# The second attention by pairs of heads: masking by a matrix product, values with tokens on the partitions

## The chip, the cores and the metric

The kernel runs on one core of one Trainium2 chip. The metric is the device time of one execution, in microseconds, as the median of several executions. Work is shared by five engines that run side by side, each in the order of its own queue: TensorE (PE in the profile, with PEld for its weight loads), VectorE (DVE), ScalarE (ACT), GpSimd (POOL) and the DMA queues that SyncE (SP) and GpSimd issue. They wait for each other by semaphores.

## The reference, cut to what matters

The program is a trunk of two decoder layers over 256 tokens of width 1024, all in float32. Layer A uses differential attention, layer B "forgetting attention" over keys, values and forget gates that were computed once between the layers. Each layer has a SwiGLU feed-forward network before and after its attention. The change concerns layer B's attention alone:

```
def forgetting_attention(h, w_q, w_o, k, v, F):
    q = (h @ w_q).reshape(b, s, B_HEADS, HEAD_DIM)       # 16 heads of 64
    ...
        decay = Fq[..., None] - F_k[:, :, None, :]       # a number per query less one per key
        logits = einsum('bqhd,bkhd->bhqk', qb, k) * scale + decay
        logits = where(causal, logits, -inf)
        p = softmax(logits)
        return einsum('bhqk,bkhd->bqhd', p, v)
    ...
    return o.reshape(b, s, B_WIDTH) @ w_o
```

The tokens are taken in two blocks of 128 queries. The first block sees 128 keys and the second 256, so a head has 384 columns of scores on 128 partitions (`QT` in line 820 holds these two stretches).

## The kernel before, in words

**Layout and number format.** Activations lie with features on the partitions and tokens in the columns. A projection is done in split form: a weight piece and an activation are each cut into a high part, rounded to the format float32r, and a low part, and `mm3` (line 398) adds three products (high by high, low by high, high by low). Such a product of 256 columns is one matmul instruction; a product of plain float32 operands is two. Weight pieces of 128 x 1024 are loaded by SyncE, rounded by ScalarE (`cp_part`, line 288; `wh` in the profile) and subtracted by VectorE (`sub_part`, line 298; `wl`).

**Order of the work.** `InOrder` (line 58) wraps TensorE, ScalarE, VectorE and SyncE: instructions of each stay in the order in which the Python code issues them. It keeps a rough clock of each engine, and by that puts weight roundings and subtractions into gaps that it expects (`fill_act`, `fill_dve`, `bg`). GpSimd is called directly.

**The stage around the change.** `late_pairs` (line 498) computes the first two tiles of queries, each with four heads (`lp` in the profile), while normalisation of the input still runs; its last steps are the normalised input `HH`, `HL`, and then the second query tile (`lcol`, `lt`, `q`) on ScalarE and VectorE. Then `attention_b` (line 1059) goes head by head, in 19 turns of a pipeline, 16 heads and three turns to empty it:

- `decay(t + 1)`: VectorE adds the query's number, the key's number (a row broadcast by DMA, `fkb`) and the causal mask, for the next head.
- `normal(t - 1)`: VectorE takes the reciprocals of the sums (`rsb`) and divides the 384 columns of weights of the previous head.
- `scores(t)`: two products of 64 rows (`sb`), on VectorE scaled logits with the decay and the maximum (`nmb`), on ScalarE exponentials with their sums.
- `weights_t(t - 2)`: three transposes of the weights (`pwb`), copied to SBUF by ScalarE into one of two buffers (`wtb`).
- `values(t - 3)`: two products with features on the partitions (`pob`), two heads in one accumulator; after the second, ScalarE rounds it (`obh`) and VectorE subtracts (`obl`).

Between these, `step(n)` gives TensorE filler work by a written plan (`PLAN`, line 45): first the projection of the other two query tiles (`pair_proj`, `pq`, six matmuls a step), then the output projection of the heads that are done (`OutProj.steps`, `pw`, three matmuls a step). In the first turns a filler stands on both sides of the scores. `op.finish` (line 697) does the last two of eight parts of the output projection and updates the residual stream; the next feed-forward network starts with `lg` and `lu`.

Accumulators are PSUM tiles with tags: `sbank` has two buffers, `abank` and `bbank` one each, `mmbank` four.

Of the kernel before, what the change touches and what calls it, by code (L numbers as in the profile page):

```python
# [10 lines left out]
F32 = mybir.dt.float32  # L11
F32R = mybir.dt.float32r
BF16 = mybir.dt.bfloat16
AF = mybir.ActivationFunctionType
ALU = mybir.AluOpType
PSUM = bass.MemoryType.PSUM

P = 128
D = 1024
S = 256  # L20
NC = D // P
HD = 64
AH = 8
BH = 16
# [5 lines left out]
BIG = 3.0e38  # L30
# [9 lines left out]
CP_FIT = 0.9  # L40
DVE_FIT = 0.6
NFILL = 1
FRONT = 0
TAIL = 4
PLAN = [1, 1, 1, 1, 2, 1, 2, 3, 1, 3]
PACE = [0.62, 0.74, 0.62, 0.38, 0.76, 0, 0.74]
NRAW = 6
NLO = 5
# [59 lines left out]
def trunk(ctx, tc, a, out):  # L108
    nc = tc.nc
    InOrder.ready = {}  # L110
    pe = InOrder(tc, nc.tensor, 0.0, 1 / 2350)
    act = InOrder(tc, nc.scalar, 0.13, 1 / 1200)
    dve = InOrder(tc, nc.vector, 0.08, 1 / 960)
    sp = InOrder(tc, nc.sync, 0.0, 1 / 704)
    cp_ = ctx.enter_context(tc.tile_pool(name="cp", bufs=1))
# [3 lines left out]
    kp = ctx.enter_context(tc.tile_pool(name="kp", bufs=2))  # L119
    pp = ctx.enter_context(tc.tile_pool(name="pp", bufs=1, space=PSUM))  # L120

    def mmbank(name):
        return pp.tile([P, 512], F32, tag="mm", name=name, bufs=4)

    def sbank(name):
        return pp.tile([P, 512], F32, tag="s", name=name, bufs=2)

    def abank(name):
        return pp.tile([P, 512], F32, tag="ta", name=name)

    def bbank(name):
        return pp.tile([P, 512], F32, tag="tb", name=name)

    mm = pe.matmul
# [248 lines left out]
    def run_laters():  # L383
        for e in list(laters):
            e[0] -= 1
            if e[0] <= 0:
                laters.remove(e)
                e[1]()
# [9 lines left out]
    def mm3(ps, w, xx, first, last):  # L398
        (wh, wl), (xh, xl) = w, xx
        mm(ps, wh, xh, start=first, stop=False, skip_group_check=True)  # L400
        mm(ps, wl, xh, start=False, stop=False, skip_group_check=True)
        mm(ps, wh, xl, start=False, stop=last, skip_group_check=True)
        work(P)
# [329 lines left out]
    def pair_proj(src, dst, name):  # L733

        pq = mmbank(name)
        blk = take(src)
        for k in range(NC):
            for b in range(2):
                mm3(pq[:, b * 256:b * 256 + 256], blk(k * 256 + b * P), hn[k],
                    k == 0 and b == 0, k == NC - 1)  # L740
            if k == NC - 1:
                act.copy(dst, pq)
            yield k, NC
# [76 lines left out]
    QT = ((0, 128), (128, 256))  # L820
# [4 lines left out]
    ident, cmask, ub, skew, nlam, subg = (late[n] for n in ("ident", "cmask", "ub", "skew", "nlam", "subg"))  # L825
# [159 lines left out]
    op = attention_a()  # L985
# [5 lines left out]
    kT = [cp_.tile([P, 512], F32, name=f"kT{j}") for j in range(4)]  # L991
    vb = [[cp_.tile([P, 512], F32, name=f"vb{t}{nh}") for nh in range(2)] for t in range(2)]
# [17 lines left out]
    pz = sbank("pzf")[:, :S]  # L1010
# [13 lines left out]
    for i, (kk, n) in enumerate(v_proj("wkv", vb)):  # L1024
# [9 lines left out]
        if i == 3:  # L1034
# [4 lines left out]
            Fq = cp_.tile([P, 72], F32, name="Fq")[:, :2 * BH]  # L1039
# [6 lines left out]
            fdram = tc.dram_tile([BH, S], F32, name="fdram")  # L1046
# [12 lines left out]
    def attention_b():  # L1059
        ohs = [cp_.tile([P, 512], F32R, tag=f"hidh{j}", name=f"obh{j}") for j in range(4)]  # L1060
        ols = [cp_.tile([P, 512], F32R, tag=f"hidl{4 + j}", name=f"obl{j}") for j in range(4)]
        o = [(ohs[c // 2][:, (c % 2) * 256:(c % 2) * 256 + 256],
              ols[c // 2][:, (c % 2) * 256:(c % 2) * 256 + 256]) for c in range(NC)]
        q = [cp_.tile([P, 512], F32, tag=f"hidl{j}", name=f"q{j}") for j in range(4)]
        gs, ds, sms = {}, {}, {}

        def load_g(hd):
            g = cp_.tile([P, S], F32, tag=("hidh10", "hidl10", "hidl8", "hidl9")[hd % 4], name=f"fkb{hd}")
            nc.gpsimd.dma_start(g, bass.AP(fdram.tensor, fdram.offset + hd * S, [[0, P], [1, S]]))
            gs[hd] = g  # L1070

        def decay(hd):
            d = cp_.tile([P, 384], F32, tag=f"hidh{4 + hd % 4}", name=f"d{hd}")
            for qt, (c0, w) in enumerate(QT):
                dve.scalar_tensor_tensor(
                    d[:, c0:c0 + w], gs[hd][:, :w], Fq[:, qt * BH + hd:qt * BH + hd + 1], cmask[:, S - w:],
                    op0=ALU.add, op1=ALU.add)
            ds[hd] = d
            if hd + 4 < BH:
                load_g(hd + 4)  # L1080

        late_pairs("wq", q[:2], ((1, 4), (1, 3)), AF.Exp)
        for hd in range(4):
            load_g(hd)
        decay(0)
        op = OutProj(o)
        st = {}
        pob = {}
        mode[0] = "fill"

        def scores(hd):
            c, m = hd // 2, hd % 2
            rows = slice(m * HD, m * HD + HD)
            cb = (c % 2) * 256
            d = ds[hd]
            s = sbank(f"sb{hd}")
            for qt, (c0, w) in enumerate(QT):
                mm(s[:, c0:c0 + w], q[c // 2][rows, cb + qt * P:cb + qt * P + P],
                   kT[c // 2][rows, cb:cb + w], start=True, stop=True)
            nm = kp.tile([P, 2], F32, tag="nm", name=f"nmb{hd}")  # L1100
            sm = kp.tile([P, 2], F32, tag="sm", name=f"smb{hd}")
            for qt, (c0, w) in enumerate(QT):
                dve.tensor_tensor_reduce(
                    d[:, c0:c0 + w], s[:, c0:c0 + w], d[:, c0:c0 + w], -0.125, BIG,
                    ALU.add, ALU.min, accum_out=nm[:, qt:qt + 1])
                act.activation(d[:, c0:c0 + w], d[:, c0:c0 + w], AF.Exp,
                               bias=nm[:, qt:qt + 1], scale=-1.0, accum_out=sm[:, qt:qt + 1])
            sms[hd] = sm

        def normal(hd):  # L1110
            d = ds[hd]
            rs = kp.tile([P, 2], F32, tag="rs", name=f"rsb{hd}")
            dve.reciprocal(rs, sms[hd])
            for qt, (c0, w) in enumerate(QT):
                dve.tensor_scalar(d[:, c0:c0 + w], d[:, c0:c0 + w], rs[:, qt:qt + 1], None, op0=ALU.mult)

        def weights_t(hd):
            pw = abank(f"pwb{hd}")
            for b in range(3):
                pe.transpose(pw[:, b * P:b * P + P], ds[hd][:, b * P:b * P + P], ident)  # L1120
            wt = cp_.tile([P, 384], F32, tag=f"hidh{8 + hd % 2}", name=f"wtb{hd}")
            act.copy(wt, pw[:, :384])
            st[hd] = wt

        def values(hd):
            c, m = hd // 2, hd % 2
            rows = slice(m * HD, m * HD + HD)
            if m == 0:
                pob[c] = bbank(f"pob{c}")
            po, wt = pob[c], st[hd]  # L1130
            vs = slice((hd % 8) * HD, (hd % 8) * HD + HD)
            v0, v1 = vb[0][hd // 8][:, vs], vb[1][hd // 8][:, vs]
            mm(po[rows, 128:256], v1, wt[:, 256:384], start=True, stop=False, skip_group_check=True)
            mm(po[rows, 0:256], v0, wt[:, 0:256], start=False, stop=True, skip_group_check=True)
            if m == 1:
                oh, ol = o[c]
                act.copy(oh, po[:, :256])
                dve.tensor_tensor(ol, po[:, :256], oh.bitcast(F32), op=ALU.subtract)

        def fills():  # L1140
            for j in (2, 3):
                yield from pair_proj("wq", q[j], f"pq{j}")
            for _ in range(6):
                yield from op.steps()

        fill = fills()

        def step(n):
            for _ in range(n):
                next(fill, None)  # L1150

        step(FRONT)
        for t in range(BH + 3):
            n0, n1 = PLAN[2 * (t // 4):2 * (t // 4) + 2]
            step(n0)
            if t + 1 < BH:
                decay(t + 1)
            if 0 <= t - 1 < BH:
                normal(t - 1)
            if t < BH:  # L1160
                scores(t)
            step(n1)
            if 0 <= t - 2 < BH:
                weights_t(t - 2)
            if 0 <= t - 3 < BH:
                values(t - 3)
        for i, n in fill:
            if i % 4 == 3:
                run_laters()
        return op  # L1170

    pace[0] = PACE[5]
    op = attention_b()
    op.finish((1, 5), ((1, 7), (1, 6)))
    pace[0] = PACE[6]
# [132 lines left out]
```

## Time and profile before

| | |
|---|---|
| median of 3 executions | 1008.04 us (1007.78 to 1008.06) |
| the profiled execution's own time | 1012.33 us |
| its span in the trace | 1010.4 us |
| TensorE busy | 98% of the span |
| VectorE, ScalarE, GpSimd busy | 81%, 56%, 4% |
| second attention, from the first filler after the late pairs to the next network's first matmul | 738.90 to 812.39 us |

Times in the rows below are microseconds from the start of the span, and the second number of a row is its duration, unless the text says otherwise. "x6" counts instructions that were merged into the row. A bracket at the end of a row gives the idle time of the engine before it and the engine and tile whose end released it. Nearly all instructions go through the wrapper, so their line is that of the wrapper, L103, and rows are told apart by the tile that they write (left of the arrow). Matmuls are pipelined, so the pace is read from start to start and not from their durations.

### The profile page before, as it was taken

The numbers are of one execution on the slowest core, as the hardware profiler recorded it, in microseconds if no ns is written. First come the engines' busy times: TensorE is split into PE (matmuls) and PEld (weight loads), VectorE is DVE, ScalarE is ACT, GpSimd is POOL, SyncE is SP. The second block draws the span as 40 slices with busy tenths as digits, with TensorE's granted clock in tenths as the row PEclk, the third lists the DMA queues.
The fourth block names the chain that finished last, engine by engine and source line by source line (L and its number), as shares of the span: only waits on it lengthen the run. The fifth ranks groups of instructions, "written<-read, shape, count | busy, mean of one in ns | idle before, by whom it ended". The sixth has DMA issues, their size and how long they took to land.

```text
span 1010.4 us, 20397 instructions
## 1 busy us (share of the span) xinstructions
PE 986.9 (98%) x8076; PEld 948.1 (94%) x8076; DVE 821.5 (81%) x1379; ACT 562.3 (56%) x922; POOL 38.1 (4%) x64
## 2 busy tenths in 40 slices
PE   6999999999999999999999999999999999999996
PEld 4999999988999999999988999999977799999996
DVE  7989979899889998888798989889897697554553
ACT  4465455576767645455566544545665585544552
POOL 0000100001111000000000000000011010000000
PEclk9999999999999999999999999999999999999999
DMA  9988999958665899788767999989743337554551
GB/s 353 414 323 301 345 368 337 363 191 321 210 225 186 268 393 349 276 292 313 262 230 276 357 349 349 334 296 346 257 121 108 126 128 230 186 188 138 173 170 42
DMA packets 68129, 265.06 MB, mean 262 GB/s; under 512 B 7961, under 2 KB 8113, under 8 KB 57922
## 3 DMA queue, kind: packets, MB, share of 16 engines
q1 hardware_dynamic: 65810, 258.31, 72.2%
q0 software_dynamic: 1792, 4.81, 1.7%
q8 instruction: 63, 1.03, 0.4%
q10 hardware_dynamic: 432, 0.64, 0.2%
q14 instruction: 32, 0.26, 0.1%
HBM read 262.66 MB, written 2.65 MB: 263 GB/s over the span
## 4 chain that ended last, share of the span: by engine, by line
PE 91%; ACT 4%; DVE 3%; issue 1%; POOL 1%; DMA 0%; SPq 0%; DVEq 0%; ACTq 0%
PE po L103 24%; PE pg L103 21%; PE pu L103 21%; PE pf L103 5%; PE pv L103 4%; PE pw L103 3%; PE lp L103 3%; PE pk L103 1%; ACT nl L103 1%; PE pob L103 1%; PE lg L103 1%; PE lu L103 1%; PE pqk L103 1%; PE sb L103 1%; ACT on L103 1%; DVE ada L103 1%
## 5 line engine op out<-in xcount | busy, mean ns | idle before, releaser
L103 DVE TENSOR_TENSOR wl<-raw,wh 128x1024 fp32r<-128x1024 f32 (+1 forms) x368 | 400.9, 1105 | 90.4 <-issue 24.3
L103 ACT CAST wh<-raw 128x1024 fp32r<-128x1024 f32 (+1 forms) x368 | 349.2, 958 | 208.1 <-PE pu L103 95.0
L103 DVE CUSTOM_DVE_ANT_0 ada<-ada,cact,vecs 128x1024 f32<-128x1024 f32 x160 | 203.6, 1279 | 0.0
L103 PE MATMUL po<-hidl,wh 128*128 128x256 f32 x704 | 195.2, 277 | 0.0
L103 PE MATMUL po<-hidh,wh 128*128 128x256 f32 x704 | 195.2, 277 | 0.0
L103 PE MATMUL po<-hidh,wl 128*128 128x256 f32 x704 | 195.2, 277 | 0.0
L103 PE MATMUL pg<-HH,wh 128*128 128x256 f32 x608 | 168.8, 278 | 0.0
L103 PE MATMUL pu<-HH,wl 128*128 128x256 f32 x608 | 168.8, 278 | 0.0
L103 PE MATMUL pg<-HL,wh 128*128 128x256 f32 x608 | 168.7, 278 | 0.0
L103 PE MATMUL pu<-HH,wh 128*128 128x256 f32 x608 | 168.7, 278 | 0.0
L103 PE MATMUL pg<-HH,wl 128*128 128x256 f32 x608 | 168.7, 277 | 0.0
L103 PE MATMUL pu<-HL,wh 128*128 128x256 f32 x608 | 168.7, 277 | 0.0
L103 PEld LDWEIGHTS po<-hidh,wl 128*128 128x128 f32 x704 | 132.9, 189 | 0.0
L103 PEld LDWEIGHTS po<-hidl,wh 128*128 128x128 f32 x704 | 132.2, 188 | 0.0
L103 PEld LDWEIGHTS po<-hidh,wh 128*128 128x128 f32 x704 | 132.2, 188 | 0.0
L103 PEld LDWEIGHTS pg<-HH,wl 128*128 128x128 f32 x608 | 114.8, 189 | 0.0
L103 PEld LDWEIGHTS pg<-HH,wh 128*128 128x128 f32 x608 | 114.2, 188 | 0.7 <-issue 0.6
L103 PEld LDWEIGHTS pu<-HH,wl 128*128 128x128 f32 x608 | 114.8, 189 | 0.0
L103 PEld LDWEIGHTS pu<-HL,wh 128*128 128x128 f32 x608 | 114.2, 188 | 0.0
L103 PEld LDWEIGHTS pu<-HH,wh 128*128 128x128 f32 x608 | 114.1, 188 | 0.0
L103 PEld LDWEIGHTS pg<-HL,wh 128*128 128x128 f32 x608 | 114.1, 188 | 0.0
L103 ACT CAST hidh<-hf 128x512 fp32r<-128x512 f32 x44 | 27.3, 621 | 45.5 <-DVE hf L103 45.5
(204 smaller groups left out, 1606.7 us busy)
## 6 DMA issues: line engine op xcount, KB each, us to landing
raw<-in_win SPq DMA_DIRECT2D x176, 512.0 KB, 6.3
ada<-in_ada SPq DMA_DIRECT2D x79, 1024.0 KB, 7.4
raw<-in_wout SPq DMA_DIRECT2D x64, 384.0 KB, 4.9
raw<-in_wout SPq DMA_DIRECT2D x64, 320.0 KB, 4.5
raw<-in_wqk SPq DMA_DIRECT2D x16, 512.0 KB, 5.7
raw<-in_wo SPq DMA_DIRECT2D x16, 512.0 KB, 4.9
raw<-in_wv SPq DMA_DIRECT2D x8, 512.0 KB, 6.8
raw<-in_wkk SPq DMA_DIRECT2D x8, 512.0 KB, 6.8
```

Source lines behind the costliest of these rows:

```text
L103: return self.tc.keep_in_program_order(f(*args, **kw))
```

## The change

The second attention now goes by pairs of heads, in 11 groups, 8 pairs and three groups to empty the pipeline. `group(t)` issues all TensorE work of four stages at once, then the work of ScalarE and VectorE on it, then the decays of the next pair, and the fillers stand behind the whole group (eight steps up to group 3, seven up to group 8, then six; a step of the query projection counts double).

- The decay, without the mask, is made by GpSimd (four `tensor_scalar` for a pair); the broadcast loads fetch two heads at once.
- The mask is added on TensorE: identity times mask, both copied once by ScalarE to float32r (`identr`, `maskr`), four products of 128 columns for a pair, into the accumulators to which the scores are then added. The scores of the two heads alternate.
- The six transposes of a pair go to two accumulators; ScalarE copies four of them, VectorE two, each into a single buffer.
- The values are products with the weights stationary, three per head with 64 moving columns, so that tokens lie on the partitions; division takes place there, in one VectorE operation per pair.
- The result is transposed back by two transposes into spare columns of the scores' accumulators, then rounded by ScalarE and subtracted by VectorE.

```diff
+        identr = cp_.tile([P, P], F32R, tag="hidl8", name="identr")
+        maskr = cp_.tile([P, P], F32R, tag="hidl9", name="maskr")
+        def load_g(c):
+            g = cp_.tile([P, 512], F32, tag=("hidh10", "hidl10")[c % 2], name=f"fkb{c}")
+            nc.gpsimd.dma_start(g, bass.AP(fdram.tensor, fdram.offset + 2 * c * S, [[0, P], [1, 2 * S]]))
+        def decay(c):
+            for m in range(2):
+                hd = 2 * c + m
+                d = cp_.tile([P, 384], F32, tag=f"hidh{4 + hd % 4}", name=f"d{hd}")
+                for qt, (c0, w) in enumerate(QT):
+                    nc.gpsimd.tensor_scalar(d[:, c0:c0 + w], gs[c][:, m * S:m * S + w],
+                                            Fq[:, qt * BH + hd:qt * BH + hd + 1], None, op0=ALU.add)
+            if c + 2 < BH // 2:
+                load_g(c + 2)
         late_pairs("wq", q[:2], ((1, 4), (1, 3)), AF.Exp)
+        act.copy(identr, ident)
+        act.copy(maskr, cmask[:, P:])
...
+        def scores(c, sb):
+            for m in range(2):
+                for qt, c0 in enumerate((0, 256)):
+                    mm(sb[m][:, c0:c0 + P], identr, maskr, start=qt == 0, stop=False, skip_group_check=True)
             for qt, (c0, w) in enumerate(QT):
+                for m in range(2):
+                    rows = slice(m * HD, m * HD + HD)
+                    mm(sb[m][:, c0:c0 + w], q[c // 2][rows, cb + qt * P:cb + qt * P + P],
+                       kT[c // 2][rows, cb:cb + w], start=False, stop=qt == 1, skip_group_check=True)
+        def weights_out(c, ta, tb):
+            w0 = cp_.tile([P, 512], F32, tag="hidh8", name=f"wta{c}")
+            w1 = cp_.tile([P, 256], F32, tag="hidh9", name=f"wtb{c}")
+            act.copy(w0, ta)
+            dve.tensor_copy(w1, tb[:, :256])
+        def values(c, po):
+            for m in range(2):
+                wt = st[c][3 * m:3 * m + 3]
+                mm(po[:, m * HD:m * HD + HD], wt[0], v0, start=True, stop=True)
+                mm(po[:, P + m * HD:P + m * HD + HD], wt[1], v0, start=True, stop=False)
+                mm(po[:, P + m * HD:P + m * HD + HD], wt[2], v1, start=False, stop=True)
+        def divide(c, po):
+            dve.reciprocal(rs, sms[c])
+            dve.tensor_tensor(on..., po..., rs... .to_broadcast([P, 4, HD]), op=ALU.mult)
+        def out_split(c, pz):
+            for qt in range(2):
+                act.copy(oh[:, qt * P:qt * P + P], pz[qt])
+            for qt in range(2):
+                dve.tensor_tensor(ol[:, qs], pz[qt], oh[:, qs].bitcast(F32), op=ALU.subtract)
+        def group(t):
+            cs, cw, cv, co = (c if 0 <= c < NP else None for c in (t, t - 1, t - 2, t - 3))
+            sb = [sbank(f"sb{t}_{m}") for m in range(2)] if cs is not None or co is not None else None
+            ta = abank(f"wa{t}") if cw is not None else None
+            tb = bbank(f"wb{t}") if cw is not None or cv is not None else None
...
+            # in this order, each where its pair exists:
+            # scores(cs), weights_t(cw), values(cv), out_t(co),
+            # weights_out(cw), divide(cv), exps(cs), out_split(co), decay(t + 1)
+        for t in range(NP + 3):
+            group(t)
+            for _ in range(8 if t < 4 else 7 if t < 9 else 6):
+                next(fill, None)
```

More of the change, by code (lines that the diff above doesn't have):

```diff
@@ L42 @@
 NFILL = 1
-FRONT = 0
 TAIL = 4
-PLAN = [1, 1, 1, 1, 2, 1, 2, 3, 1, 3]
 PACE = [0.62, 0.74, 0.62, 0.38, 0.76, 0, 0.74]
@@ L1065, in attention_b @@
         gs, ds, sms = {}, {}, {}
[L1067 to L1080, printed above, removed]
+        identr = cp_.tile([P, P], F32R, tag="hidl8", name="identr")
[3 more added lines that the diff above has]
+            nc.gpsimd.dma_start(g, bass.AP(fdram.tensor, fdram.offset + 2 * c * S, [[0, P], [1, 2 * S]]))
+            gs[c] = g
+        def decay(c):
[5 more added lines that the diff above has]
+                                            Fq[:, qt * BH + hd:qt * BH + hd + 1], None, op0=ALU.add)
+                ds[hd] = d
+            if c + 2 < BH // 2:
+                load_g(c + 2)
         late_pairs("wq", q[:2], ((1, 4), (1, 3)), AF.Exp)
-        for hd in range(4):
-            load_g(hd)
+        act.copy(identr, ident)
+        act.copy(maskr, cmask[:, P:])
+        for c in range(2):
+            load_g(c)
         decay(0)
@@ L1087, in attention_b @@
         st = {}
-        pob = {}
         mode[0] = "fill"
-        def scores(hd):
-            c, m = hd // 2, hd % 2
-            rows = slice(m * HD, m * HD + HD)
+        NP = BH // 2
+        def scores(c, sb):
             cb = (c % 2) * 256
-            d = ds[hd]
-            s = sbank(f"sb{hd}")
+            for m in range(2):
+                for qt, c0 in enumerate((0, 256)):
+                    mm(sb[m][:, c0:c0 + P], identr, maskr, start=qt == 0, stop=False, skip_group_check=True)
@@ L1097, in scores @@
             for qt, (c0, w) in enumerate(QT):
[L1098 to L1138, printed above, removed]
+                for m in range(2):
+                    rows = slice(m * HD, m * HD + HD)
+                    mm(sb[m][:, c0:c0 + w], q[c // 2][rows, cb + qt * P:cb + qt * P + P],
+                       kT[c // 2][rows, cb:cb + w], start=False, stop=qt == 1, skip_group_check=True)
@@ new lines, in exps @@
+        def exps(c, sb):
+            nm = kp.tile([P, 4], F32, tag="nm", name=f"nmb{c}")
+            sm = kp.tile([P, 4], F32, tag="sm", name=f"smb{c}")
+            for m in range(2):
+                d = ds[2 * c + m]
+                for qt, (c0, w) in enumerate(QT):
+                    cc = 2 * qt + m
+                    dve.tensor_tensor_reduce(
+                        d[:, c0:c0 + w], sb[m][:, c0:c0 + w], d[:, c0:c0 + w], -0.125, BIG,
+                        ALU.add, ALU.min, accum_out=nm[:, cc:cc + 1])
+                    act.activation(d[:, c0:c0 + w], d[:, c0:c0 + w], AF.Exp,
+                                   bias=nm[:, cc:cc + 1], scale=-1.0, accum_out=sm[:, cc:cc + 1])
+            sms[c] = sm
@@ new lines, in weights_t @@
+        def weights_t(c, ta, tb):
+            for j in range(6):
+                d, b = ds[2 * c + j // 3], j % 3
+                pe.transpose(ta[:, j * P:j * P + P] if j < 4 else tb[:, (j - 4) * P:(j - 3) * P],
+                             d[:, b * P:b * P + P], ident)
+        def weights_out(c, ta, tb):
[3 more added lines that the diff above has]
+            dve.tensor_copy(w1, tb[:, :256])
+            st[c] = [w0[:, j * P:j * P + P] for j in range(4)] + [w1[:, j * P:j * P + P] for j in range(2)]
@@ new lines, in values @@
+        def values(c, po):
+            for m in range(2):
+                hd = 2 * c + m
+                wt = st[c][3 * m:3 * m + 3]
+                vs = slice((hd % 8) * HD, (hd % 8) * HD + HD)
+                v0, v1 = vb[0][hd // 8][:, vs], vb[1][hd // 8][:, vs]
+                mm(po[:, m * HD:m * HD + HD], wt[0], v0, start=True, stop=True)
+                mm(po[:, P + m * HD:P + m * HD + HD], wt[1], v0, start=True, stop=False)
+                mm(po[:, P + m * HD:P + m * HD + HD], wt[2], v1, start=False, stop=True)
@@ new lines, in divide, with out_t @@
+        def divide(c, po):
+            rs = kp.tile([P, 4], F32, tag="rs", name=f"rsb{c}")
+            dve.reciprocal(rs, sms[c])
+            on = kp.tile([P, 256], F32, tag="w512b", name=f"onb{c}")
+            dve.tensor_tensor(on.rearrange("p (g d) -> p g d", g=4), po.rearrange("p (g d) -> p g d", g=4),
+                              rs.rearrange("p (g o) -> p g o", o=1).to_broadcast([P, 4, HD]), op=ALU.mult)
+            st[c] = on
+        def out_t(c, pz):
+            for qt in range(2):
+                pe.transpose(pz[qt], st[c][:, qt * P:qt * P + P], ident)
@@ new lines, in out_split @@
+        def out_split(c, pz):
+            oh, ol = o[c]
+            for qt in range(2):
+                act.copy(oh[:, qt * P:qt * P + P], pz[qt])
+            for qt in range(2):
+                qs = slice(qt * P, qt * P + P)
+                dve.tensor_tensor(ol[:, qs], pz[qt], oh[:, qs].bitcast(F32), op=ALU.subtract)
[4 more added lines that the diff above has]
+            tb = bbank(f"wb{t}") if cw is not None or cv is not None else None
+            if cs is not None:
+                scores(cs, sb)
+            if cw is not None:
+                weights_t(cw, ta, tb)
+            if cv is not None:
+                values(cv, tb[:, 256:])
+            if co is not None:
+                pz = [sb[m][:, 384:] for m in range(2)]
+                out_t(co, pz)
+            if cw is not None:
+                weights_out(cw, ta, tb)
+            if cv is not None:
+                divide(cv, tb[:, 256:])
+            if cs is not None:
+                exps(cs, sb)
+            if co is not None:
+                out_split(co, pz)
+            if t + 1 < NP:
+                decay(t + 1)
@@ L1140, in fills @@
         def fills():
             for j in (2, 3):
-                yield from pair_proj("wq", q[j], f"pq{j}")
+                for _ in pair_proj("wq", q[j], f"pq{j}"):
+                    yield
+                    yield
             for _ in range(6):
-                yield from op.steps()
+                for _ in op.steps():
+                    yield
         fill = fills()
-        def step(n):
-            for _ in range(n):
+        for t in range(NP + 3):
+            group(t)
+            for _ in range(8 if t < 4 else 7 if t < 9 else 6):
@@ L1150, in step @@
                 next(fill, None)
[L1152 to L1169, printed above, removed]
+        for _ in fill:
+            pass
```

## The prediction

> **What bounds the kernel now.** I read the page first: its table of busy time, then its chain of work that ended last.
>
> ```profile
> PE 986.9 (98%) x8076; PEld 948.1 (94%) x8076; DVE 821.5 (81%) x1379; ACT 562.3 (56%) x922; POOL 38.1 (4%) x64
> ...
> PE 91%; ACT 4%; DVE 3%; issue 1%; POOL 1%; DMA 0%; SPq 0%; DVEq 0%; ACTq 0%
> ```
>
> TensorE carries 91% of the chain. So what counts is TensorE time in the second attention, and every moment in which TensorE waits there. I therefore asked next for the engines' busy time in stretches around its beginning.
>
> ```profile
> 740.00:745.00 5.00, 4.59 (x32) 3.60 (x30) 4.69 (x14) 3.12 (x8) 0.30 (x1) 1.00 0.00 0
> 745.00:750.00 5.00, 4.33 (x29) 3.54 (x29) 4.83 (x25) 4.77 (x14) 2.02 (x4) 1.00 0.41 79
> 750.00:755.00 5.00, 4.47 (x29) 3.13 (x27) 4.82 (x19) 3.99 (x13) 1.07 (x2) 1.00 0.45 102
> 755.00:760.00 5.00, 5.00 (x31) 3.57 (x31) 4.23 (x16) 2.60 (x10) 0.58 (x2) 1.00 0.60 208
> ```
>
> The columns after the length are PE, PEld, DVE, ACT, POOL, clock and DMA. TensorE is short of work by 0.4 to 0.7 us per 5 us from 740 to 755, when VectorE is nearly full, and full from 755 on. The chain of waits shows the steady state, and the end of the stage:
>
> ```profile
> 778.39 0.85 PE sb L103 x4
> 779.24 0.56 PE pw L103 x3
> 779.80 0.33 PE pwb L103 x3
> 780.13 0.79 PE pob L103 x4
> 780.92 0.90 PE pw L103 x6
> 781.83 0.85 PE sb L103 x4
> ...
> 797.35 1.58 PE pw L103 x12
> ...
> 805.13 7.26 PE pw L103 x60
> 812.39 0.73 PE lg L103 x4
> ```
>
> From one sb to the next (778.39 to 781.83) is one head with nine filler matmuls (pw): 3.44 us. Twelve fillers take 1.58 and six 0.90, so one more costs 0.113, and in the last block 60 take 7.26, 0.121 each; I use 0.115. A head is 3.44 - 9 x 0.115 = **2.4 us** of TensorE: scores 0.85, three transposes 0.33, values 0.79, and some 0.4 of slower first fillers after a block (0.90 for six instead of 6 x 0.115 = 0.69, twice a head).
>
> The stage runs from 738.90, the first matmul after the late pairs, to 812.39: 73.5 us. Its work is 16 x 2.4 = 38.2 and 288 fillers (16 steps of six, 48 of three, 48 in the finish) x 0.115 = 33.1, so 71.3; some 2.2 us are waits.
>
> **Part 1, TensorE work per pair.** Removed are 2 x 2.4 = 4.78 us. What comes in has near relatives in the first attention, which already scores two half-height groups side by side, and in a small product of 16 columns:
>
> ```profile
> 262.33 0.91 PE s L103 x8
> ...
> 263.55 1.87 ACT nl L103 x8
> ...
> 528.63 0.74 PE L103 MATMUL pF<-lft,tri 128*128 128x16 f32 x6
> ...
> 529.29 0.82 PE L103 MATMUL pFk<-tri,lft 128*16 128x128 f32 x4
> ```
>
> - *Scores*: eight instructions for two heads in 0.91, against four for one head in 0.85 before. The two row halves run at once. With the slow entry and exit seen above, about 1.06.
> - *Six transposes*: 6 x 0.11 = 0.65, as before.
> - *Values*: twelve instructions (three products a head, two each) of 64 columns against full 128-column weights. Six with only 16 columns took 529.29 - 528.63 = 0.66, so 0.11 each whatever the columns: the weight load sets it. 12 x 0.112 = 1.34, against 1.58 before.
> - *Two output transposes*: 0.22.
> - *Four mask products* in float32r of 128 columns: not in the trace. Below, half of a 256-column filler, 0.057; above, what a float32 product of 128 columns costs (two instructions of 0.11), 0.22. I take 0.113, the weight-load pace of the nearest row (pF): 0.45. Both ends are kept: -1.8 and +3.4 us over eight pairs.
>
> Sum 3.72 us, so TensorE gains 1.06 a pair, **8.4 us** in all.
>
> [...]
>
> **Part 2, the front.** Before, TensorE went from the late pairs straight into fillers of the third q tile, which need nothing new. The change puts group 0 first, and its first instructions need the two constants that ScalarE copies, written behind everything of the late pairs on ScalarE's in-order queue:
>
> ```profile
> 738.78 0.28 PE L103 MATMUL lp<-HL,wh 128*128 128x258 f32 x1
> 738.90 0.28 PE L103 MATMUL pq<-HH,wh 128*128 128x256 f32 x1
> ...
> 742.47 0.20 ACT L103 COPY lcol<-lp 128x1 f32<-128x1 f32 x2
> 743.51 0.91 ACT L103 ACTIVATE q<-lt,lcol 128x256 f32<-128x256 f32 x2 [0.84 <-DVE lt L103]
> 744.33 1.03 ACT L103 CAST wh<-raw 128x1024 fp32r<-128x1024 f32 x1
> ```
>
> Nothing ahead of that changes, so the copies start where the weight cast stands now, 744.33, and take about 0.45 for both (between the 0.10 a copy of the one-column lcol and 0.37 for 128x256 below). TensorE can start the mask at about 744.85: **5.95 us idle** from 738.90, where before it did 30 fillers and two heads' scores. The decay of pair 0 is hidden: GpSimd can make it while the late pairs run. This wait replaces the old front's 2.2 us of waits.
>
> **Part 3, the loop.** Two accumulators hold a pair's scores, and the next group's mask may not be written before this group's last reader of them, the subtraction in out_split. Also, the transposed weights now have one buffer each where there were two, so their copies wait until TensorE has finished the values of the pair before. Prices for the rest of that chain:
>
> ```profile
> 785.07 0.37 ACT L103 CAST obh<-pob 128x256 fp32r<-128x256 f32 x1 [0.26 <-PE pob L103]
> ...
> 785.48 0.43 DVE L103 TENSOR_TENSOR obl<-pob,obh 128x256 fp32r<-128x256 f32 x1 [0.98 <-ACT obh L103]
> 785.82 0.74 DVE L103 SCALAR_TENSOR_TENSOR d<-fkb,Fq,tri 128x128 f32<-128x128 f32 x2
> 786.47 0.16 DVE L103 RECIPROCAL rsb<-smb 128x2 f32<-128x2 f32 x1
> 786.66 0.55 DVE L103 TENSOR_SCALAR d<-d,rsb 128x128 f32<-128x128 f32 x2
> 787.13 0.28 DVE L103 CUSTOM_DVE_ANT_0 d<-sb,d 128x128 f32<-128x128 f32 x1
> ...
> 787.52 0.41 ACT L103 ACTIVATE d<-d,nmb 128x128 f32<-128x128 f32 x1 [1.13 <-DVE nmb L103]
> ```
>
> From the first mask product: mask, scores, transposes and values 3.50, results visible 3.7; copy of w1 0.35 (785.48 to 785.82, the step of a 128x256 operation), reciprocal 0.19, division 0.35: 4.6; first maximum to first exponential 0.39 (787.13 to 787.52): 5.0; four exponentials with their sums 1.87 (row nl): 6.85; two half-width casts 0.45: 7.3; last subtraction about 0.3: **7.6 us**. TensorE's own work is 3.72 + 21 x 0.115 = 6.14 (24 fillers, 6.48, in group 3). Out_split exists from group 3 on, scores until group 7: groups 3 to 6 wait 1.1 + 3 x 1.46 = 5.5, and group 8's transposes wait for the exponentials of group 7 (6.9 against 6.14) 0.8: **6.3 us**. Behind the waiting mask stand the transposes and values of the older pairs and the fillers, as TensorE takes all in order. Bounds: 3 if the casts and copies overlap better (without the buffer wait the chain is 0.5 shorter), 9 if a 1.2 us weight split slips into each chain.
>
> VectorE loses 16 decays (0.66) and 16 divisions of the weights, but in these groups it is late by order, not by load. GpSimd takes four operations a pair; its nearest row:
>
> ```profile
> L442 POOL TENSOR_TENSOR acc<-sq,sq 128x256 f32<-128x256 f32 x2 | 1.6, 808 | 44.9 <-ACT sq L103 44.9
> ...
> L1069 POOL DMA_DIRECT2D fkb<-fdram x16 | 8.9, 556 | 234.8 <-PE po L103 194.2 <-DVE rsb L103 23.4 <-DVE d L103 16.6
> ```
>
> At up to 0.8 each, with one load issue (0.56) instead of two, that is 3.8 us. They may begin once the transposes of their old tile are through (2.2 into the group) and are wanted 4.6 into the next, 10 us later. Cost nothing; without that cover every us would go into the loop.
>
> **Part 4, the clock.** TensorE has idled for several us only at the ends of the kernel:
>
> ```profile
> 14.70 0.58 PE L103 MATMUL pf<-HH,wh 128*128 128x256 f32 x1 [3.75 <-ACT HH L103]
> ...
> 17.99 0.41 PE L103 MATMUL pf<-HH,wh 128*128 128x256 f32 x1
> 18.21 0.41 PE L103 MATMUL pf<-HH,wl 128*128 128x256 f32 x1
> ...
> 19.05 0.28 PE L103 MATMUL pf<-HL,wh 128*128 128x256 f32 x1
> 19.17 0.28 PE L103 MATMUL pf<-HH,wh 128*128 128x256 f32 x1
> ...
> 1001.44 0.70 PE L103 MATMUL psn<-sq,ones 128*128 128x256 f32 x2 [0.59 <-ACT sq L103]
> ...
> 1005.00:1010.00 5.00, 0.00 (x0) 0.00 (x0) 1.61 (x3) 0.00 (x0) 0.00 (x0) 0.55 0.57 210
> ```
>
> After the last matmul (ending 1002.14) a mean clock of 0.55 over 1005 to 1010 (full for 0.5 us, half for 4.5) means half clock from about 1005.5, so 3.4 us of idleness were enough. At the start, matmuls stand 0.22 apart until 19.05 and 0.12 after, 4.35 us after work began at 14.70. An idle front of 5.7 us (738.78 + 0.28 to 744.85) should thus bring half clock, and 4.35 us at half speed lose **2.2 us** of fully TensorE-bound time (0 to 3.4).
>
> [...]
>
> **Sum.** After: fillers 33.1 + pairs 8 x 3.72 = 29.8 + front 5.95 + loop 6.3 + slower finish 0.4 (60 x 0.006, there before too) = 75.5, against 73.5: +2.0. With the clock: +4.2. The profiled execution took 1012.33 us (span 1010.4), the median of the runs is 1008.04; the difference is put on the median: **1012.2 us**.
>
> **Rivals.**
> - *The clock stays up* (25%): all as above, 1008.04 + 2.0 = 1010.0. For it: 5.7 us is not far above 3.4. Against: every idle time of 3.4 us and more here was cold after.
> - *The loop does not bind* (16%): casts and division overlap the fillers, TensorE stays full, and its 8.4 us come home: 8.4 + 2.2 (old waits) - 5.95 - 0.8 (group 8) = 3.9 less, 1004.1; 1006.3 with the cold clock. It decides once the chain behind the values takes less than the 2.6 us of output transposes and fillers. Against: the rows add to 3.9.
> - *Mask products at float32 price, 0.22* (12%): 0.43 more in each of eight groups, loop included: 1008.04 + 4.2 + 3.4 = 1015.6.
> - *The decays do not hide* (4%): the loop then takes GpSimd's time; four operations of 2.5 us and an issue are 10.6 a group, 3.0 more in seven groups: 1033. Against: the 0.81 row.
>
> **How the numbers follow.** The forecast has 43%. The range reaches into the faster case and to the dear mask: 1005.5 to 1016. The likeliest case's own range, from the bounds of the loop (3 to 9) and the clock, is 1008.5 to 1015. What a measurement of this kernel tells from no change is about 0.2%, 2.0 us: below 1006.0 lies most of the second rival (15%); between 1006.0 and 1010.1 the rest of it, half of the first and the low end of the forecast, 25%; above, 60%.
>
> **What would show it.** An idle TensorE from about 739 to 745 ended by ScalarE's copy of a constant; a granted clock below 1 behind it; eight scores in 0.9 us; twelve values in 1.3; mask products 0.11 apart; waits of 1 to 1.5 us ahead of the mask in groups 4 to 7, ended by VectorE's subtraction. I am wrong if TensorE finds work in the front, or if those waits are missing.

## The result, and the profile after

The changed kernel is slower. Its median is 1016.21 us (1008.83 to 1019.87, 20 runs), against 1007.74 us (1006.39 to 1013.93, 20 runs) of the kernel before on the same chip. The ratio is **1.0059, with a 95% interval of 1.0042 to 1.0077**: 4.2 to 7.8 us more. The quotient of the medians, 1.0084, is larger, and that of the means is 1.0061, because the times lie in two groups: 7 from 1008.83 to 1010.61 and 13 from 1015.08 to 1019.87 for the changed kernel, 17 from 1006.39 to 1010.21 and 3 from 1012.75 to 1013.93 for that of before. The profiled execution took 1018.39 us (span 1016.5); that of before took 1012.33 (span 1010.4).

From the page of the changed kernel, the table of busy time (share of the span, instructions):

```profile
PE 980.6 (96%) x8156; PEld 953.8 (94%) x8156; DVE 808.1 (79%) x1331; ACT 559.4 (55%) x924; POOL 60.1 (6%) x88
```

TensorE has 6.3 us less work than before (986.9) in a span 6.1 us longer: it waits 12 us more. The chain of waits of the changed kernel shows where (start, length, engine, tile; some steps left out):

```profile
748.51 0.19 ACT identr L101
748.70 0.21 ACT maskr L101
748.95 2.70 PE sb L101 x12
...
755.53 1.25 PE sb L101 x12
...
773.53 1.49 PE sb L101 x12
...
775.60 1.52 PE wb L101 x14
777.15 0.42 DVE wtb L101
...
778.03 0.28 DVE d L101
...
778.36 1.87 ACT d L101 x8
780.23 0.16 ACT obh L101
780.41 0.30 DVE obl L101
780.85 1.49 PE sb L101 x12
```

Two things are new. At the front TensorE takes up its work only after ScalarE's two copies of constants, and its first twelve instructions of `sb` then take 2.70 us, where a group later they take 1.25. In the loop (773.53 to 780.85) the chain leaves TensorE after the values and goes through VectorE, ScalarE, ScalarE again and VectorE before it comes back to the next mask.

The waits of the changed kernel between 740 and 822 (idle time of TensorE ahead of a tile and what ended it: sum in us, count, longest):

```profile
PE sb L101 <- ACT maskr L101: 6.7, 1, 6.7
...
PE sb L101 <- DVE obl L101: 3.8, 4, 1.1
```

The same kernel in stretches (length, then PE, PEld, DVE, ACT, POOL, granted clock, DMA share and GB/s):

```profile
746.00:746.80 0.80, 0.00 (x0) 0.00 (x0) 0.56 (x3) 0.61 (x3) 0.19 (x1) 0.99 0.00 0
746.80:753.60 6.80, 4.65 (x21) 3.88 (x22) 3.98 (x13) 3.72 (x12) 0.00 (x0) 0.50 0.42 116
753.60:755.00 1.40, 1.40 (x14) 1.40 (x13) 0.53 (x1) 1.33 (x3) 0.00 (x0) 1.00 0.00 0
```

The granted clock falls to half while TensorE still waits, and is full again 6.8 us later, of which TensorE worked 4.65; before, it was 1.00 throughout here.

For all comparisons below, **the stage** is the time from the start of the last matmul of the late pairs to the first of the next network. Here are these two matmuls in the timeline of the changed kernel, and others that are used further down (start, length, engine, operation; in brackets the idle time before it and what ended it):

```profile
736.77 4.06 POOL L1079 TENSOR_SCALAR d<-fkb,Fq 128x128 f32<-128x128 f32 x4 [5.38 <-DMA fkb<-fdram]
741.77 3.54 POOL L1079 TENSOR_SCALAR d<-fkb,Fq 128x128 f32<-128x128 f32 x4
742.02 0.28 PE L101 MATMUL lp<-HL,wh 128*128 128x258 f32 x1
742.69 0.69 DVE L101 SCALAR_TENSOR_TENSOR HL<-ht,modall,HH 128x256 fp32r<-128x256 f32 x1
745.97 0.48 DVE L101 SCALAR_TENSOR_TENSOR HL<-ht,modall,HH 128x256 fp32r<-128x256 f32 x1
775.67 2.98 POOL L1079 TENSOR_SCALAR d<-fkb,Fq 128x128 f32<-128x128 f32 x4 [3.46 <-issue]
776.75 0.59 ACT L101 COPY wta<-wa 128x512 f32<-128x512 f32 x1 [3.06 <-PE wb L101]
777.09 0.36 PE L101 MATMUL pw<-obh,wh 128*128 128x256 f32 x1
777.15 0.42 DVE L101 COPY wtb<-wb 128x256 f32<-128x256 f32 x1 [2.44 <-PE wb L101]
777.29 0.28 PE L101 MATMUL pw<-obh,wl 128*128 128x256 f32 x1
779.53 0.28 PE L101 MATMUL pw<-obl,wh 128*128 128x256 f32 x1
818.11 0.28 PE L101 MATMUL lg<-HH,wh 128*128 128x258 f32 x1
```

The stage took 73.45 us before (738.78 to 812.23) and takes 76.09 now (742.02 to 818.11): 2.6 us more. That is less than the ratio. Of the 6.1 us between the two spans, 3.2 us had come up before the stage began (742.02 against 738.78), and 3.0 of these at the very start of the program: the first product `psn` starts at 12.76 us, against 9.72.

### The profile page after: what moved, and what is told of

It reads as the page before. It is cut to its first block, busy times and chain, and to the rows that moved or that the text cites. A ratio compares the mean times of both kernels' runs of the same rounds, so it can differ in the third digit from the quotient of the medians.

```text
span 1016.5 us, 20544 instructions
## 1 busy us (share of the span) xinstructions
PE 980.6 (96%) x8156; PEld 953.8 (94%) x8156; DVE 808.1 (79%) x1331; ACT 559.4 (55%) x924; POOL 60.1 (6%) x88
## 3 DMA queue, kind: packets, MB, share of 16 engines
q8 instruction: 64, 1.05, 0.4%
## 4 chain that ended last, share of the span: by engine, by line
PE 89%; ACT 4%; DVE 4%; issue 1%; DMA 1%; POOL 1%; SPq 0%; DVEq 0%; ACTq 0%
PE po L101 24%; PE pg L101 21%; PE pu L101 21%; PE pf L101 5%; PE pv L101 4%; PE lp L101 3%; PE pw L101 2%; PE sb L101 1%; PE pk L101 1%; ACT nl L101 1%; PE wb L101 1%; PE lu L101 1%; PE lg L101 1%; PE pqk L101 1%; PE pq L101 1%
```

## The experiments

The two theories were these. **A**, as in the prediction: the loop waits because the transposed weights have one buffer, and because the next mask stands behind the subtraction of `out_split`. **B**: the buffers make no difference, and it is only the order in which ScalarE and VectorE work off the group (the exponentials ahead of `out_split`). For the front: ScalarE's copies are the whole wait, and the half clock follows from it. All stages measured, with the waits of TensorE ahead of groups 4 to 7 that VectorE's subtraction `obl` ended:

| kernel | stage, us | waits of TensorE for `obl`, us | median, us (runs) | ratio to before, 95% |
|---|---|---|---|---|
| before | 73.45 | | | |
| changed | 76.09 | 0.68, 1.04, 1.03, 1.09 | 1016.21 (20) | 1.0059 (1.0042 to 1.0077) |
| again | 76.16 | 0.68, 1.06, 1.03, 1.03 | 1012.84 (12) | 1.0053 (1.0025 to 1.0080) |
| early | 71.63 | 0.75, 1.04, 1.03, 1.03 | 1009.21 (12) | 0.9995 (0.9967 to 1.0022) |
| swap | 72.02 | none | 1008.77 (12) | 1.0003 (0.9978 to 1.0029) |
| early_swap | 65.32 | none | 1004.42 (12) | 0.9946 (0.9916 to 0.9975) |
| warm | 74.03 | 0.68, 1.05, 1.02, 1.03 | 1013.03 (1) | |
| two_buffers | 77.94 | 0.82, 1.09, 1.17, 1.09 | 1019.84 (1) | |
| mask_on_vector | 69.14 | 0.59, 0.94, 1.33, 1.00 | 1005.72 (10) | 0.9945 (0.9921 to 0.9968) |
| mask_on_vector_swap | 65.22 | none | 1002.93 (7) | 0.9907 (0.9871 to 0.9942) |

The kernel before had a median of 1008.11 us beside again, early, swap and early_swap, and 1012.98 beside the last four, of which warm and two_buffers ran once. So medians of different sets are not to be compared, but ratios are.

**again: the changed kernel unchanged**, as the base of its set.

> The changed kernel once more, nothing edited. [...] The profiled execution of the changed kernel also began its late pairs 3.2 us later than that of the kernel before (729.8 against 726.6), ahead of everything that was changed. If that is chance, this profile may as well begin them at 726 to 727, and its times spread as the old kernel's do; rival: the change itself moves the start, and it is 3 us late again while the old kernel's is not.

The stage took 76.16 us, where 76 to 77.5 had been expected and 0.07 more than in the first trace, with the same front and the same loop. The ratio, 1.0053 (1.0025 to 1.0080), agrees with the first. So the stage repeats within 0.1 us, and the 4.2 to 7.8 us of the first comparison is not an accident of its set. The stage began late here too, with the last matmul of the late pairs at 742.03 us. The expectation named that as the sign that the change itself moves the start. But warm, which differs from the changed kernel only behind the late pairs, has this matmul at 738.82, and before has it at 738.78, so the late start is not bound to the change.

**early: the constants are copied ahead of the late pairs**, into a buffer that is free by then.

```
+        im = kp.tile([P, 512], F32R, tag="w512a", name="im")
+        identr, maskr = im[:, :P], im[:, P:2 * P]
+        act.copy(identr, ident)
+        act.copy(maskr, cmask[:, P:])
         late_pairs("wq", q[:2], ((1, 4), (1, 3)), AF.Exp)
-        act.copy(identr, ident)
-        act.copy(maskr, cmask[:, P:])
```

> The two constants are copied to float32r ahead of the late pairs (into a free buffer), so the first mask product waits for nothing new. [...] Rival (the decays on GpSimd are what is late): the front stays as long, ended by VectorE or GpSimd, and under 1 us is won.

Waits of early, timeline, and stretches (PE, clock, DMA share and GB/s):

```profile
PE sb L101 <- DVE obl L101: 3.9, 4, 1.0
...
PE sb L101 <- DVE nmb L101: 1.9, 1, 1.9
```

```profile
747.27 0.96 PE L101 MATMUL sb<-im 128*128 128x128 f32 x4 [1.94 <-DVE nmb L101]
```

```profile
745.00:750.00 5.00, 2.91 (x18) 0.86 0.26 58
750.00:755.00 5.00, 5.00 (x39) 0.80 0.31 99
```

The wait for `maskr` is gone, and the stage is 4.5 us shorter, not the 6.5 expected. Once TensorE may start, it runs through the scores of group 0 and its eight fillers and then stands 1.94 us ahead of group 1, which needs the maxima of group 0; VectorE makes these behind the late pairs. Some 3 us of such a stop had been expected. Most of the rest is the clock, which had been expected to stay up and fell all the same: its means of 0.86 and 0.80 in the two stretches are half clock from 748.6 to 752.0, 3.4 us, or some 1.7 us of work. ScalarE's copies were thus not the whole wait of the front. The loop's waits are unchanged, so front and loop are separate losses.

**swap: `out_split` is written ahead of the exponentials.**

```
+            if co is not None:
+                out_split(co, pz)
             if cs is not None:
                 exps(cs, sb)
-            if co is not None:
-                out_split(co, pz)
```

> In each group the rounding and subtraction of the finished pair stand ahead of the exponentials instead of behind them. Theory: the accumulators come free after the last maximum, some 6.3 us into a group that holds 6.0 us of TensorE work, so the four waits of 0.7 to 1.1 us (3.8 us together) shrink to 0.3 or less: 3 us less than the changed kernel; front and clock as they were. Rival (the exponentials come late and hold the next transposes): the waits move from the mask to the transposes, and the time stays.

The chain of waits of swap, one group:

```profile
775.07 1.25 PE sb L101 x12
776.33 0.59 PE wa L101 x4
776.91 1.50 PE wb L101 x14
778.42 0.23 PE sb L101 x2
778.65 2.48 PE pw L101 x21
781.12 1.25 PE sb L101 x12
```

and TensorE's waits in swap from 735 to 822:

```profile
PE sb L101 <- ACT maskr L101: 6.6, 1, 6.6
PE wb L101 <- ACT d L101: 0.2, 1, 0.2
```

All four waits for the subtraction are gone (the 0.2 us that is left stands in group 8), and a group takes 6.05 us (775.07 to 781.12), all of it TensorE's own work, where it took 7.32. The stage is 4.1 us shorter, 3 were expected. The buffers are as in the changed kernel. So one buffer for the transposed weights is enough, and what made the loop wait is that the two roundings and two subtractions stood behind 1.87 us of exponentials on in-order queues. The chip's result is even with the kernel before, 1.0003 (0.9978 to 1.0029).

**early_swap: both.**

> Both edits. Theory: they add up, 6.5 + 3 = 9.5 us less than the changed kernel, 6 us less than the kernel before (0.6%). Rival: they overlap, since a loop without waits meets VectorE's or GpSimd's own time, and no more than early alone is won.

Waits and stretches of early_swap (columns of all engines in the stretches):

```profile
PE sb L101 <- DVE nmb L101: 2.0, 1, 2.0
```

```profile
745.00:750.00 5.00, 4.23 (x35) 3.74 (x36) 3.70 (x18) 3.98 (x16) 1.89 (x3) 1.00 0.34 108
```

The stage is 10.8 us shorter (9.5 expected, 6.5 of it for early, which measured 4.5), 2.2 more than 4.5 + 4.1; most of that is the clock, which stayed at 1.00 here and cost early some 1.7. The kernel beats the kernel before: 0.9946 (0.9916 to 0.9975).

**warm: seven products in the idle front.** They keep TensorE busy while it waits; their result is read by nobody.

```
         late_pairs("wq", q[:2], ((1, 4), (1, 3)), AF.Exp)
+        dm = mmbank("dm")
+        for _ in range(7):
+            mm(dm, kT[0][:, :P], vb[0][0], start=True, stop=True)
```

> Seven float32 products of 512 columns, of operands that are long ready, into an accumulator that nobody reads, are put into the idle time before group 0 (nothing else changes; they are extra work and no part of the result). Theory: TensorE is kept active until about 748, so the granted clock stays at full speed behind the idle time, and group 0 with its fillers takes 4.2 us instead of 6.6: the stage from the late pairs' last matmul to the next network's first is 2.3 us shorter, 73.7 instead of 76.0 us. Rival: the slow first group comes from something else (the constants, the first exponentials, weights that are late), and the stage stays at 76.

Timeline and stretch (PE, clock, DMA share and GB/s) of warm:

```profile
738.94 6.17 PE L101 MATMUL dm<-vb,kT 128*128 128x512 f32 x14
...
745.66 0.66 PE L101 MATMUL sb<-maskr,identr 128*128 128x128 f32 x4 [0.55 <-ACT maskr L101]
```

```profile
745.00:750.00 5.00, 4.45 (x37) 1.00 0.32 105
```

The mask still waits for the same copy, and the loop's waits are the same 3.8 us in all; what differs is the clock. The stage is 2.1 us shorter than in again (74.03 against 76.16). That is the price of the half clock, to a few tenths, since the pace of the fillers varies too (last section).

**two_buffers: two buffers for the transposed weights**, so that no copy waits for the values of the pair before.

```
-            w0 = cp_.tile([P, 512], F32, tag="hidh8", name=f"wta{c}")
-            w1 = cp_.tile([P, 256], F32, tag="hidh9", name=f"wtb{c}")
+            w0 = cp_.tile([P, 512], F32, tag=("hidh8", "hidl8")[c % 2], name=f"wta{c}")
+            w1 = cp_.tile([P, 256], F32, tag=("hidh9", "hidl9")[c % 2], name=f"wtb{c}")
```

(The constants move to the buffer that early uses, but are still copied behind the late pairs.)

> The copies of the transposed weights get two buffers each instead of one (the constants move to another buffer, still copied behind the late pairs). The prediction held that these copies wait for the single buffer. Theory A: they do, then VectorE's copy starts right behind the transposes, 1.3 us earlier in the group, the division waits for the values alone, and each of the four loop waits is 0.4 to 0.5 us shorter: 1.8 us in all. Theory B: VectorE's copy waits anyway, because its accumulator also takes the values and is not read while TensorE writes to it; then only ScalarE's copy starts earlier, which is not on the chain, and the waits stay at 0.7 and 1.0.

Chain, waits and timeline of two_buffers:

```profile
774.75 1.49 PE sb L101 x12
```

```profile
PE sb L101 <- DVE obl L101: 4.2, 4, 1.2
```

```profile
776.86 0.58 ACT L101 COPY wta<-wa 128x512 f32<-128x512 f32 x1 [1.94 <-PE wa L101]
778.37 0.42 DVE L101 COPY wtb<-wb 128x256 f32<-128x256 f32 x1 [2.43 <-PE wb L101]
```

The loop waits as long as with one buffer: 4.2 us against 3.8. ScalarE's copy `wta` does start earlier, 2.11 us after the group's first instruction (774.75 to 776.86) where it was 3.22 (773.53 to 776.75). VectorE's copy `wtb` starts 3.62 us after it in both kernels (774.75 to 778.37, 773.53 to 777.15), its wait ended by TensorE's `wb` in both. Only the second lies on the chain. So the buffer of `wta` was a true wait, but off the path, and the half of theory A that rests on the buffers falls. What holds `wtb` is left: the values of the older pair go into the other half of the accumulator from which `wtb` is copied, and their instructions come last in it. That this sharing is the reason was argued, not tried. The stage was even longer, 77.94 us. The loop's waits are 0.4 of these 1.9 us; the mean granted clock of the profiled execution was 0.992, against 0.993 in the changed kernel's, but how much of the rest is the clock was not shown.

**mask_on_vector: the mask goes back into the decay on VectorE**, so that TensorE needs no mask products and no constants, and GpSimd no decays. The pairs stay.

```
-                    nc.gpsimd.tensor_scalar(d[...], gs[c][...], Fq[...], None, op0=ALU.add)
+                    dve.scalar_tensor_tensor(d[...], gs[c][...], Fq[...], cmask[:, S - w:],
+                                             op0=ALU.add, op1=ALU.add)
...
-        act.copy(identr, ident)
-        act.copy(maskr, cmask[:, P:])
...
-                    mm(sb[m][:, c0:c0 + P], identr, maskr, start=qt == 0, stop=False, ...)
...
-                       kT[...], start=False, stop=qt == 1, ...)
+                       kT[...], start=True, stop=True)
```

> The decay is made by VectorE again with the mask in the same operation (four operations of some 0.35 us per pair); the mask product, the two constants and GpSimd's decays are gone; the pairs, the values and the division stay. Theory: the front has nothing to wait for (as with the early constants: 4.5 us, and the clock stays up), TensorE saves 8 x 0.45 = 3.6 us of mask products in the groups where TensorE is the bound and in the chain of the loop alike, VectorE's late pairs are not slowed by GpSimd; 8 us less than the changed kernel's stage of 76.0, so 68. Rival: with the decays VectorE is late in the loop and the waits grow by 1.4 us in each of four groups, which gives half of it back: 73.

Timeline of mask_on_vector:

```profile
740.54 0.48 DVE L101 SCALAR_TENSOR_TENSOR HL<-ht,modall,HH 128x256 fp32r<-128x256 f32 x1
...
743.24 1.40 DVE L101 SCALAR_TENSOR_TENSOR d<-fkb,Fq,tri 128x128 f32<-128x128 f32 x4
```

The stage is 69.14 us, 7.0 less than in again (68 was expected). The decays cost VectorE 1.40 us for four at the front, and the loop waits for the same subtraction as in the changed kernel, 3.9 us in all. The clock did not stay up as expected: after a stop of 2.8 us ahead of group 1, its means were 0.97 from 742 to 747 and 0.69 from 747 to 752, which is half clock from 746.7 to 750.1.

**mask_on_vector_swap: the same with `out_split` first.**

> The same, and the rounding and subtraction of the finished pair ahead of the exponentials. Theory: loop waits gone as well, TensorE is the bound from group 1 on: the stage of the two edits before (65.2 us) less 8 x 0.45 of mask products, 61.6 to 62.5 us; about 11 us (1.1%) faster than the kernel before. Rival: VectorE, with four more operations in a group, now sets the pace of the loop: 65 us or more, with waits for its maxima ahead of the scores.

Waits and stretches (all engines) of mask_on_vector_swap:

```profile
PE sb L101 <- DVE nmb L101: 2.8, 1, 2.8
```

```profile
750.00:755.00 5.00, 4.07 (x20) 3.42 (x21) 3.71 (x19) 3.31 (x12) 1.07 (x2) 0.71 0.30 84
```

The loop is full, as in swap, and the stage 65.22 us, against 61.6 to 62.5 expected. What was missed is the front: 2.8 us of waiting for the maxima of group 0, behind the late pairs on VectorE, where early_swap waited 2.0, and 3.4 us of half clock after it (0.71 in that stretch, 0.95 in the next 5 us). The rival's 65 us is met, but not by its reason, as no wait is left in the loop. The time is 0.9907 of before (0.9871 to 0.9942). This and early_swap are the best two; their intervals overlap, so which is better is open.

## Why the prediction was right or wrong

The forecast of 1012.2 us and its sign held, and most of its mechanism, but how near the time came is in part luck, as the stage grew less than forecast and the rest came from outside it: 1.0059 of the 1008.04 us shown is 1014.0 (1012.3 to 1015.8), inside the range of 1005.5 to 1016.0; the median by itself, 1016.21, is just above that range.

**TensorE's work per pair: right.** The trace of the changed kernel has 3.56 us from the first mask product of a group to its first filler (773.53 to 777.09), and 3.72 were forecast. Mask and scores take 1.25 together in a group that does not start from a stop (755.53), the transposes 0.109 each, the values 0.112 each and the mask products 0.112 each, where the prediction had taken 0.11, 0.112 and 0.113. Values of 64 columns do cost as much as the earlier row of 16 columns (0.112 and 0.11). That the weight load sets this pace was the prediction's reading of that row, where each of the six matmuls has a weight load of its own; no run tried it. The gain of about 1 us a pair, 8 us in all, was really there: swap and early together, which take nothing from that work, got it home (65.32 against 73.45).

**The front: right in kind, 0.9 us too short.** TensorE stood 6.65 us, ended by `maskr`. From the start of the last matmul of the late pairs to the first mask product 6.93 us passed (742.02 to 748.95), and the forecast's rows give 6.07 for that (738.78 to 744.85). The prediction's step "Nothing ahead of that changes" failed. GpSimd's decays of the first pairs ran from 736.77 to 745.3, beside the late pairs. In that time VectorE's `HL` took up to 0.70 where it takes 0.48 once GpSimd is done (742.69 and 745.97 in the timeline above), and GpSimd's four took 4.06 and 3.54, where in the loop four took 3.72 once and then 2.98 or 2.99. From the start of the late pairs' last matmul to that of the last two `lt` were 5.07 us, against 4.22 before and 4.24 in mask_on_vector, which has the same late pairs and no decays on GpSimd. So "cost nothing" held in the loop, where at most 3.72 + 0.58 us a group lies under TensorE's work, and not at the front. The 2.2 us of old waits, which the prediction had as the remainder of its sum, are 1.6 in its own rows (0.41, 0.67 and 0.53 short of 5 us from 740 to 755); that leaves the forecast as it is, but makes the second rival 0.6 us dearer.

**The loop: right in place and size of the chain, wrong in a reason, too dear in the sum.** The chain was forecast at 7.6 us and measured 7.32; the waits of groups 4 to 7 were ended by the subtraction, as said. Their sum is 0.68 + 1.04 + 1.03 + 1.09 = 3.84 us, against 5.5. Group 8's wait of 0.8 does not exist. The 0.5 us that the step "their copies wait until TensorE has finished the values" put on the single buffer is refuted by two_buffers. The subtraction behind the exponentials is the cause, as swap shows: with these two moved, none of the 3.84 us is left.

**The clock: right.** 2.2 us were forecast, and warm gives 2.1. The half clock ran 6.8 us, from 746.8 to 753.6, and began in a stop of 6.7; in early it ran 3.4 us, after one of 1.94.

**The sum: right in sign.** The stage grew by 2.6 and 2.7 us in two traces, where +4.2 was forecast. Against the forecast the front is 0.9 longer, the loop's waits are 1.7 and group 8's 0.8 shorter, and the pairs 8 x 0.16 = 1.3 shorter: that gives 1.3. Two terms at the seams between fillers and groups were missing. The first filler after each of eleven groups takes 0.20 (777.09 to 777.29) where 0.115 was costed: 0.9 more. And each of the four waits counts from the end of the last filler, 0.28 after its start (779.53 + 0.28 + 1.04 = 780.85), where again 0.115 was costed: 0.7 more. With these the sum is 2.9, which is 0.2 to 0.3 above the two traces. The fillers in between go at 0.118 in some groups (19 steps from 777.29 to 779.53) and at 0.114 in others (757.78 to 760.05), 0.115 in the mean, as costed. The measured 4.2 to 7.8 us is more than the stage. The rest lies outside the changed code and **stays open**. One thing there does vary. The stretch from 860 to 880 lies in the last network, with TensorE busy at full clock throughout; the first profile of the changed kernel (first fence) and that of again (second), the same kernel, with PE, clock, DMA share and GB/s:

```profile
860.00:880.00 20.00, 20.00 (x173) 1.00 0.60 192
```

```profile
860.00:880.00 20.00, 20.00 (x179) 1.00 0.61 197
```

173 matmuls in the one, 179 in the other, of the same form. In the first trace the network's matmuls from `pg` to `po` go at 117.8 ns each (831.04 to 1006.24); for the second the two counts give an estimated 113.9 (117.8 x 173 / 179). From the first `lg` to the end of the span it is 198.2 to 198.5 us in some traces (before, changed, warm, two_buffers) and 191.9 to 192.2 in others (again, early, swap, early_swap, both with the mask on VectorE). The pace is not tied to the kernel: the changed kernel has both. The 6.3 us between the paces are of the size of the distance between the two groups of times in the first comparison (7.7 us between the means of the changed kernel's, 5.7 of before's), and the lower groups of the two kernels differ by only 2.0 us in the mean (1009.7 against 1007.7), near the 2.6 us that the stage grew. So it may be that the rest of the ratio is the slow pace coming in 13 of 20 executions instead of 3. That is inferred, not shown, as only one execution of each was traced there, and why the change should make the slow pace more frequent is open.

**The rivals.** That the loop does not bind fell on the 3.84 us; swap is the kernel that this rival described, and its 1.0003 is still above the 1006.3 that the rival gave for it with the clock cold. The dear mask fell on 0.112. The decays that do not hide fell on 2.98 us for four, against 10 a group. The clock that stays up fell in both traces of the changed kernel: 0.50 from 746.8 to 753.6 in the first, and in again the first twelve `sb` take 2.70 us as well.

## What to carry to other kernels

Where a group's last step frees the accumulator that the next group starts with, write that step ahead of the long work of its own queues; the order of two lines was worth 4.1 us here. A constant that the first instruction of a stage needs is to be made before the stage that precedes it, not at the seam. Ask of each engine to which work is given away what its neighbours pay while it works, and not only whether its own time is covered.

## What the runs showed of the hardware that was not expected

**The clock fell after stops much shorter than the front's.** In early TensorE stood only 1.94 us (fence above), was busy for 2.91 of the 5 us from 745 to 750, and ran 3.4 us at half from 748.6. In again it happened in quite another place, after a stop of 1.24 us. Timeline and stretch (all engines) of again:

```profile
509.63 0.38 PE L101 MATMUL pk<-HH,wh 128*128 128x256 f32 x1 [1.24 <-ACT HH L101]
```

```profile
510.00:515.00 5.00, 4.98 (x28) 4.70 (x27) 4.79 (x12) 2.54 (x5) 0.00 (x0) 0.66 0.31 111
```

TensorE is busy throughout that stretch with a mean clock of 0.66; in the 5 us before it, at 1.00, it was busy for 3.76. In early_swap a stop of 2.0 us brought nothing: the clock was 1.00 from 740 to 755, with TensorE busy for 3.59 of the first 5 us and 4.23 of the next. So neither the length of the stop (a fall after 1.24 us, none after 2.0) nor the busy share of such 5 us (a fall after 3.76, none after 3.59) orders these cases. What does was not shown.

**GpSimd and VectorE were both slower side by side.** At the front of the changed kernel `HL` took up to 0.70 us on VectorE beside GpSimd's decays, and 0.48 to 0.49 in mask_on_vector, which has none; four decays took 4.06 us there and 2.98 in most groups of the loop.

**The same matmul has two paces at full clock**, 117.8 and an estimated 113.9 ns in the last network, and they differ between executions of one kernel: 6.3 us, about as much as the two kernels differ. In the second attention of the changed kernel the fillers have both within a stage: 0.114 us from 757.78, 0.118 from 777.29 (above).
